# Attention weights times values: three fp32r passes on split operands instead of one fp32 matmul

## The chip, the cores and the metric

The kernel runs on one core of one Trainium2 chip. The metric is the device time of one execution in microseconds, the median of three runs.

## The reference

A backbone of two layers (DEPTH 2) over 1024 latent tokens and 256 context tokens, model width 1024, all in fp32. A layer norms and modulates the tokens, projects them, and runs three mixers side by side: attention, a Hyena long convolution and gated linear attention. Each head of each mixer is RMS-normed, all are concatenated and projected, and a SwiGLU follows. The attention has 8 query heads of 64 on 2 key/value heads:

```python
s = jnp.einsum('bqkgd,bskd->bkgqs', qg, k, preferred_element_type=jnp.float32)
p = jax.nn.softmax(s, axis=-1).astype(v.dtype)
o = jnp.einsum('bkgqs,bskd->bqkgd', p, v)
```

Latent queries read all 1280 keys, context queries the 256 context keys. In the last layer context queries aren't needed. What follows is `head_rms_norm` of `o`, so a common factor of a head's output matters only through the norm's epsilon.

## The kernel before

Each layer has three phases. Phase 1 norms, projects and prepares the mixers' inputs (queries, keys and values go to DRAM). Phase 2 (line 1372) runs the mixers. Phases 3 and 4 are the output projection and the SwiGLU. Instructions are not issued in the order of the source: a planner that simulates the engines sets each engine's order, with the tiles' dependencies and their buffers as limits. The source of phase 2 has the hyena first, then the linear attention, then the attention; the planner puts attention work among the other two.

The attention (lines 994 to 1104) goes job by job. A job is a key/value head (`kvh`), a pair of query heads (`pr`) and a block of queries: 512, 512, or 256 of the context. Layer 0 has 12 jobs, layer 1 has 8, all those of kv head 0 before those of kv head 1. `attn_kv` (line 995) loads the keys of one kv head and splits them: a high part in fp32r (an fp32 format with a shorter mantissa, which the matmul takes in one pass) and a low remainder. Kv head 0 is loaded at the end of phase 1 (line 770), kv head 1 when the first job needs it, into the pool `attn1`, which is open from the start of phase 2. `attn_q` splits the queries and finds each query's score maximum with extra matmuls and DVE reductions (line 1032). `attn_o` (line 1040) is the inner loop: per chunk of 128 keys and head, two fp32r matmuls make the scores (K1 with Q1, K2 with Q2), ACT takes the exponential (line 1057), and one plain fp32 matmul multiplies by the values (line 1060). The two heads' outputs go to partitions 0 to 63 and 64 to 127 of one PSUM bank. GpSimd adds the weights of all chunks (line 1068); after the last chunk fp32 matmuls with ones sum those over the partitions (line 1095). The block's end copies the output, squares it and the sums, adds them on DVE and norms (`headnorm`, line 977).

PSUM has eight banks, given to roles (line 1380): score maxima (0, 1, 2), scores (3, 4), outputs, sums and mean squares (5), the hyena and the linear attention (6, 7). Pools of SBUF are stacked on two sides. The right side holds `attn1`, `hna`, and on top of these the hyena's head norms `hn`; the hyena's other tiles are on the left. A pool opened later takes the room of one that has closed, and its tiles wait for the tiles that lay there.

Matmuls are all recorded at line 175, transposes at 184, low parts at 187.

Of the kernel before, what the change touches and what calls it, by code (L numbers as in the profile page):

```python
# [9 lines left out]
F32 = mybir.dt.float32  # L10
# [4 lines left out]
ALU = mybir.AluOpType  # L15
# [15 lines left out]
# columns of the combined input projection  # L31
C_Q, C_K, C_V, C_HY, C_GQ, C_GK, C_GV, C_GR, C_GF = 0, 512, 640, 768, 1536, 1664, 1792, 2048, 2304

# rows of the packed per-layer vectors
# [3 lines left out]
# ---------------------------------------------------------------- constants that depend on shapes alone  # L38
# [13 lines left out]
def _pk(m):  # L52
    """[T, K] -> [2, 128, T/128 * K]: exact parts, rows on partitions."""
    t, k = m.shape
    return np.stack([x.reshape(t // P, P, k).transpose(1, 0, 2).reshape(P, -1) for x in _hilo(m)])


def _consts():
# [27 lines left out]
    # rotations from the half-sample offset to offset 0, frequencies on partitions  # L86
# [37 lines left out]
class Builder:  # L124
# [21 lines left out]
    def ps(self, role=None):  # L146
        """a bank of PSUM: of a role, or of the current roles in turn."""
# [8 lines left out]
    def roles(self, *banks):  # L156
        """the banks of PSUM that each role takes in turn."""
        self.banks, self.turn = banks, [-1] * len(banks)

    def act_table(self, name):  # L160
        """one activation table set from here on: ScalarE's later instructions stay behind its load."""
# [11 lines left out]
    # -------------------------------------------------------------- small helpers  # L173
# [3 lines left out]
    def mm3(self, out, w, x, start, stop):  # L177
        """w, x: pairs (hi, lo); out += whi xhi + whi xlo + wlo xhi."""
        self.mm(out, w[0], x[0], start, False)
        self.mm(out, w[0], x[1], False, False)  # L180
        self.mm(out, w[1], x[0], False, stop)
# [7 lines left out]
    def rsqrt(self, pool, v, n, tag, eps=None, bufs=2):  # L189
        """-2 / sqrt(v + eps) for v [128, n] in PSUM: exp(-ln/2) and a Newton step."""  # L190
# [13 lines left out]
    # -------------------------------------------------------------- setup  # L204
# [42 lines left out]
    def vectors(self, vp, silb, ahead):  # L247
        """the conditioning vectors, biases and gains, features on partitions; other loads go ahead in between."""
        nc, A = self.nc, self.A
        for srcs in ((("c", None, 8), ("c_ctx", None, 8)),  # L250
# [22 lines left out]
            elif "filt_b1" in at:  # L273
                nc.vector.tensor_copy(self.fvec, ps[:, 0:3])
                # the norm gains scaled by -1/2: rsqrt() returns -2 / sqrt
# [6 lines left out]
    # -------------------------------------------------------------- adaLN vectors  # L282
# [10 lines left out]
    def ada_pe(self, l, part, wp, silb, ahead=()):  # L293
        """mod vectors: the conditioning vectors (16 columns each) stationary, weights moving; the rows of weights in
        turn on three column tiles."""
# [20 lines left out]
    def ada_dve(self, l, part, half, wp):  # L316
        """mod vectors of half a part: weighted rows summed on the vector engine; returns what sums the partitions."""
# [27 lines left out]
    # -------------------------------------------------------------- modulated norm: u (hi, lo) per block of tokens  # L345
    def norm_scale(self, l, which):
        """[128, 8, 2] gains: -1/2 g (1 + scale)."""
# [8 lines left out]
    def square(self, h, k, n, tp, acc):  # L356
        """adds the squares of chunk k of h [128, 8, n]; returns the sum so far, and whole, 1 / rms: tokens on partitions."""
# [23 lines left out]
    def spread(self, r, n, tp):  # L381
        """r [128, n / 128] -> -2 r of each token on all partitions, in PSUM."""
# [7 lines left out]
    def norm_u(self, h, u, scale, shift, r, tp, pool=(), tags=("s", "acc")):  # L390
        """u [128, 2, 8, n] F32R from h [128, 8, n]; r: -2 / rms; pool: the chunks whose low parts GpSimd makes."""
# [14 lines left out]
    # -------------------------------------------------------------- weights  # L406
    def load_w(self, src, n=P, wp=None, raws=None, lo_eng=None):
        """src [1024, n] -> (hi, lo) tile [128, 2, 8, n]."""
# [15 lines left out]
    # -------------------------------------------------------------- tokens in: feature-major residual  # L424
    def load_h(self, hp, xp):
        """features on partitions; yields after each block, with its -2 / rms on all partitions (PSUM)."""
# [35 lines left out]
    # -------------------------------------------------------------- hyena filters  # L462
    def sin_arg(self, pool, ps, b, fr, n):
        """sin(fr * (ps + b)) [128, n], the argument brought to [-pi, pi]."""
# [13 lines left out]
    def filter_mlp(self, fp, up):  # L478
        """hidden features of both layers' filters (a layer on 64 partitions), latent and context lengths, to DRAM."""
# [28 lines left out]
    def filter_body(self, l, kinds, fp):  # L508
        """spectra of one layer's filters to DRAM, latent ('l') and context ('c') lengths."""
# [5 lines left out]
        # X = [h_hi; h_lo], W1 = [w_hi; w_hi], W2 = w_lo  # L515
# [9 lines left out]
        def times(job):  # L525
            """the filter of a job in time, taken apart into folded levels."""
# [36 lines left out]
        def spectra(job, levels):  # L563
# [3 lines left out]
            for group in self.groups(levels):  # L567
                for pair, ps in self.transform(group, dft, fp):
                    for i, (L, k) in enumerate(pair):
# [20 lines left out]
                        else:  # L590
                            # cosine twice, or the two of the cyclic level; then the sine of either
# [26 lines left out]
    def start(self, hp, sp, up, tp, u):  # L618
        """tokens in, the first modulation vectors, the hidden features of the filters, the first norm."""
# [38 lines left out]
    # -------------------------------------------------------------- input projection  # L658
    def phase1(self, l):
        """norm 1, the input projection and what follows it token by token."""  # L660
# [3 lines left out]
        with ExitStack() as es:  # L664
# [27 lines left out]
            # feature-major columns  # L692
# [11 lines left out]
            # hyena: short convolution  # L704
# [21 lines left out]
            # gated linear attention: gates (silu as x sigmoid(x)), queries, keys  # L726
# [31 lines left out]
            with self.pool("t1q", 2, reuse_waits="tile") as tp:  # L758
# [5 lines left out]
                self.V = self.t(ap, [P, 10, P], F32, "V", 1)  # L764
                nc.sync.dma_start(out=self.V, in_=self.v_d)
# [8 lines left out]
    def open_w(self):  # L774
        """room of the streamed weights."""
# [8 lines left out]
    def open_u0(self):  # L784
        """room of the first block of the normed tokens."""
# [833 lines left out]
```

## Time and profile before

| | |
|---|---|
| median of three runs | 3708.47 us |
| lowest, highest | 3706.87, 3712.83 us |
| span of the profiled execution | 3712.2 us |
| PE busy | 3563.2 us (96%) |
| DVE busy | 2014.1 us (54%) |
| POOL busy | 1353.5 us (36%) |
| ACT busy | 1088.0 us (29%) |

No time of the profiled execution is given beside its span. A busy share is a mean over stages with different limits. PE is TensorE, PEld its weight loads, DVE VectorE, ACT ScalarE, POOL GpSimd, SP the engine that issues most DMAs. A plain fp32 matmul shows as two records.

### The profile page before, as it was taken

What the parts mean: (1) busy time and instruction counts of PE and PEld (TensorE: products, weight loads), DVE (VectorE), ACT (ScalarE), POOL (GpSimd) and SP (SyncE); (2) the same over time, 40 slices, a digit from 0 to 9 for tenths busy, and PEclk for the clock granted to TensorE, in tenths of its full rate; (3) what the DMA queues carried; (4) which work ended last, traced back from release to release, by engine and by line L of the source; (5) the groups of instructions that cost most, each with busy time, mean ns of one, the idle gap of its engine ahead of it and who ended that gap; (6) DMA issues with size and microseconds to landing.
All of it is one profiled execution on the core that took longest, in us unless ns stands there. A gap on an engine that the chain in (4) does not pass through costs nothing.

```text
span 3712.2 us, 46254 instructions
## 1 busy us (share of the span) xinstructions
PE 3563.2 (96%) x17903; PEld 2693.5 (73%) x17903; DVE 2014.1 (54%) x3271; ACT 1088.0 (29%) x1956; POOL 1353.5 (36%) x960
## 2 busy tenths in 40 slices
PE   8999899999999999999999899899999999999999
PEld 4789845445677888888888688865445788888887
DVE  6755667863677665644223773757753533223233
ACT  4243233553422111111111333333554421111112
POOL 2424564664333111111111541656764542221221
PEclk9999999999999999999999899999999999999999
DMA  9333311120633323321111333411112421111111
GB/s 329 99 124 123 120 33 43 56 81 20 212 110 99 95 80 89 90 66 54 49 35 46 107 111 116 150 49 42 35 70 71 139 63 51 40 57 46 52 40 57
DMA packets 275804, 310.63 MB, mean 84 GB/s; under 512 B 18680, under 2 KB 205727, under 8 KB 274304
## 3 DMA queue, kind: packets, MB, share of 16 engines
q1 hardware_dynamic: 269279, 287.75, 24.6%
q0 software_dynamic: 2560, 13.89, 1.0%
q10 hardware_dynamic: 3744, 6.03, 0.4%
q8 instruction: 140, 2.29, 0.3%
q14 instruction: 81, 0.66, 0.1%
HBM read 245.75 MB, written 61.87 MB: 83 GB/s over the span
## 4 chain that ended last, share of the span: by engine, by line
PE 75%; DVE 11%; POOL 4%; issue 3%; DMA 3%; ACT 1%; SPq 0%; DVEq 0%; POOLq 0%; ACTq 0%
PE ps L175 74%; PE ps L184 1%; POOL hss L928 1%; DMA nsq<-in_ada_w 1%; POOL hl L187 1%; DVE acc L329 1%; DVE mx L1032 1%; DVE sg L1138 1%; DMA yr<-y_d 0%; DVE h L1537 0%; POOL hy L936 0%; DVE sg L1150 0%; DVE sg L1151 0%; DVE nacc L365 0%; DVE hx L930 0%
## 5 line engine op out<-in xcount | busy, mean ns | idle before, releaser
L175 PE MATMUL ps<-u,hl 128*128 128x512 f32 (+1 forms) x6504 | 1384.4, 372 | 20.6 <-DVE u L403 6.2
L175 PEld LDWEIGHTS ps<-u,hl 128*128 128x128 f32 x6504 | 1136.3, 190 | 252.5 <-issue 14.9
L187 POOL TENSOR_TENSOR hl<-raw,hl 128x1024 fp32r<-128x1024 f32 x148 | 366.5, 2479 | 944.3 <-ACT hl L421 924.5
L175 PE MATMUL ps<-g,w 128*128 128x512 f32 (+1 forms) x2688 | 556.6, 367 | 10.0 <-DVE h L1537 3.4
L175 PEld LDWEIGHTS ps<-g,w 128*128 128x128 f32 x2688 | 466.6, 190 | 95.5 <-DVE h L1537 5.4
L1068 POOL TENSOR_TENSOR ac<-ac,p 128x512 f32<-128x512 f32 x256 | 354.7, 1394 | 159.4 <-ACT p L1057 158.8
L1498 DVE TENSOR_TENSOR s<-ps,s 128x512 f32<-128x512 f32 (+1 forms) x110 | 70.0, 637 | 614.7 <-PE ps L175 597.3
L1537 DVE SCALAR_TENSOR_TENSOR h<-ps,mod,h 128x512 f32<-128x512 f32 (+1 forms) x448 | 303.5, 687 | 181.8 <-PE ps L175 181.6
L175 PE MATMUL ps<-p,V 128*64 128x512 f32 x672 | 309.8, 607 | 4.7 <-ACT p L1057 2.5
L187 POOL TENSOR_TENSOR w<-raw,w 128x1024 fp32r<-128x1024 f32 x44 | 109.0, 2477 | 500.0 <-ACT w L421 499.9
L1032 DVE TENSOR_REDUCE mx<-ps 128x1 f32<-128x512 f32 (+1 forms) x400 | 221.0, 587 | 120.8 <-PE ps L175 119.8
L1057 ACT ACTIVATE p<-ps 128x512 f32<-128x512 f32 (+1 forms) x336 | 194.6, 586 | 286.8 <-PE ps L175 277.7
L175 PEld LDWEIGHTS ps<-Q,K 65*128 65x128 f32 (+1 forms) x672 | 105.0, 191 | 222.2 <-issue 209.8
L421 ACT CAST hl<-raw 128x1024 fp32r<-128x1024 f32 x148 | 154.9, 1049 | 303.9 <-PE ps L175 151.5
L329 DVE SCALAR_TENSOR_TENSOR acc<-nsq,silc,acc 128x512 f32<-128x512 f32 x252 | 210.6, 876 | 61.3 <-DMA nsq<-in_ada_w 60.6
L175 PE MATMUL ps<-Q,K 65*128 65x512 f32 (+1 forms) x672 | 242.2, 442 | 1.2 <-ACT p L1057 1.1
L175 PE MATMUL ps<-y,hl 128*128 128x512 f32 (+1 forms) x960 | 213.8, 381 | 13.2 <-DVE y L187 6.1
L175 PEld LDWEIGHTS ps<-y,hl 128*128 128x128 f32 x960 | 170.8, 194 | 59.3 <-DVE y L187 8.2
L421 ACT CAST w<-raw 128x1024 fp32r<-128x1024 f32 x44 | 46.2, 1051 | 491.8 <-PE ps L175 443.2
L175 PE MATMUL ps<-my,dft 128*128 128x256 f32 (+1 forms) x1176 | 166.8, 294 | 10.3 <-DVE my L187 9.7
L1499 ACT CAST g<-s 128x512 fp32r<-128x512 f32 (+1 forms) x110 | 63.3, 576 | 385.2 <-DVE s L1498 385.2
L175 PEld LDWEIGHTS ps<-my,dft 128*128 128x128 f32 x1176 | 159.1, 203 | 20.6 <-DVE my L187 13.7
(265 smaller groups left out, 4129.2 us busy)
## 6 DMA issues: line engine op xcount, KB each, us to landing
raw<-in_ffn_w SPq DMA_DIRECT2D x132, 512.0 KB
nsq<-in_ada_w SPq DMA_DIRECT2D x144, 256.0 KB
raw<-in_w_in SPq DMA_DIRECT2D x36, 512.0 KB
raw<-in_w_out SPq DMA_DIRECT2D x32, 512.0 KB
ada<-in_ada_w SPq DMA_DIRECT2D x24, 512.0 KB
h_d<-h SPq DMA_DIRECT2D x32, 256.0 KB
dft<-in_c_dft POOLq DMA_DIRECT2D x8, 1024.0 KB, 7.2
qd<-qT_d SPq DMA_DIRECT2D x64, 128.0 KB
```

The source lines that it names most:

```text
L175: self.nc.tensor.matmul(out, w, x, start=start, stop=stop)
L184: self.nc.tensor.transpose(out, in_, self.ident[:n, :n])
L187: eng.tensor_tensor(out=out, in0=x, in1=hi.bitcast(F32), op=ALU.subtract)
L329: nc.vector.scalar_tensor_tensor(out=acc[w], in0=raw, scalar=s, in1=acc[w], op0=ALU.mult, op1=ALU.add)
L421: self.nc.scalar.copy(hi, raw)
L928: nc.gpsimd.tensor_tensor(out=ss, in0=ss, in1=self.mh[:, :nh], op=ALU.pow)
L1032: nc.vector.tensor_reduce(out=mx[:, j, i:i + 1], in_=pm, op=ALU.max, axis=AX.X)
L1057: nc.scalar.activation(p, st, AF.Exp)
L1068: nc.gpsimd.tensor_tensor(out=acc[j], in0=x, in1=ps[j], op=ALU.add)
L1498: nc.vector.tensor_tensor(out=s, in0=p3, in1=s, op=ALU.mult)
L1499: nc.scalar.copy(gs[m][:, 0, o:o + n], s)
L1537: nc.vector.scalar_tensor_tensor(out=h, in0=ps, scalar=self.mod[l][:, 40 + k, w:w + 1], in1=h, op0=ALU.mult, op1=ALU.add)
```

## The change

The weights p are split: ACT copies p to an fp32r tile `ph`, GpSimd subtracts to give the low part `pl`. The values are split once a layer, into two tiles of 192 columns: the values of kv head 0, then 64 columns that hold ones in the high tile and zeros in the low one, then the values of kv head 1. A stationary operand of 128 columns is values beside ones (for kv head 1 ones beside values). Three fp32r passes accumulate, high by high, low values by high weights, high values by low weights, into one bank per head, whose other 64 partitions are the sum of the weights. GpSimd's sums and the ones matmuls are gone. The banks become (0, 1), (2, 3), (4, 5), (6, 7); the mean squares use role 0. The keys of kv head 1 go to a new pool `attn2`, opened after the hyena's pools have closed. Load buffers `qd` are two instead of three. The rest of the diff removes comments.

```diff
-                self.V = self.t(ap, [P, 10, P], F32, "V", 1)
-                nc.sync.dma_start(out=self.V, in_=self.v_d)
+                self.V = [self.t(ap, [P, 10, 192], F32R, f"V{i}", 1) for i in range(2)]
+                for i in range(2):
+                    nc.gpsimd.memset(self.V[i][:, :, 64:P].bitcast(F32), 1.0 - i)
+                for side, c in ((0, 0), (P, 64)):
+                    hi, lo = (x[:, :, side:side + 64] for x in self.V)
+                    for k in (0, 5):
+                        raw = self.t(ap, [P, 512], F32, "qd", 2)[:, :320].rearrange("p (k c) -> p k c", k=5)
+                        nc.sync.dma_start(out=raw, in_=self.v_d[:, k:k + 5, c:c + 64])
+                        self.split(raw, hi[:, k:k + 5], lo[:, k:k + 5], nc.vector)
...
-            raw = self.t(self.ap0, [P, 512], F32, "qd", 3)[:, :n]
+            raw = self.t(self.ap0, [P, 512], F32, "qd", 2)[:, :n]
...
-        return K1, K2, self.V[:, :, 64 * kvh:64 * kvh + 64]
+        return K1, K2, [x[:, :, 64 * kvh:64 * kvh + P] for x in self.V]
...
-        X = self.ps(2)[:, :n]
+        X = [self.ps(2)[:, :n] for _ in range(2)]
         k0 = 0 if b < 2 else 8
-        acc = [None, None]
...
-                p = self.t(ap, [P, 512], F32, "p", 6)[:, :n]
+                p = self.t(ap, [P, 512], F32, "p", 3)[:, :n]
+                hi, lo = (self.t(ap, [P, 512], F32R, x, i)[:, :n] for x, i in (("ph", 4), ("pl", 3)))
                 nc.scalar.activation(p, st, AF.Exp)
-                ps.append(p)
+                nc.scalar.copy(hi, p)
+                self.lo(nc.gpsimd, lo, p, hi)
+                ps.append((hi, lo))
             for j in range(2):
-                self.mm(X[64 * j:64 * j + 64], V[:, kc], ps[j], kc == k0, kc == 9)
+                self.mm(X[j], V[0][:, kc], ps[j][0], kc == k0, False)
+                self.mm(X[j], V[1][:, kc], ps[j][0], False, False)
             for j in range(2):
-                if kc == k0:
-                    acc[j] = ps[j]
-                    continue
-                x = acc[j]
-                if kc == k0 + 1:
-                    acc[j] = self.t(ap, [P, 512], F32, "ac", 2)[:, :n]
-                nc.gpsimd.tensor_tensor(out=acc[j], in0=x, in1=ps[j], op=ALU.add)
-        return X, acc
+                self.mm(X[j], V[0][:, kc], ps[j][1], False, kc == 9)
+        return X
...
-                ops[kvh] = self.attn_kv(ap, kvh)
+                ops[kvh] = self.attn_kv(self.ap1, kvh)
...
-            ps = self.ps(2)[:, :n]
+            ot = self.t(ap, [P, 512], F32, "ao", 2)[:, :n]
+            sq, e = (self.t(ap, [P, 512], F32, "sq", 2)[:, :n] for _ in range(2))
+            o, t = slice(64 * kvh, 64 * kvh + 64), slice(64 - 64 * kvh, P - 64 * kvh)
             for j in range(2):
-                self.mm(ps[64 * j:64 * j + 64], self.ones[:, :64], acc[j], True, True)
-            ot = self.t(ap, [P, 512], F32, "ao", 2)[:, :n]
-            nc.scalar.copy(ot, X)
-            sq, e = (self.t(ap, [P, 512], F32, "sq", 2)[:, :n] for _ in range(2))
+                h = slice(64 * j, 64 * j + 64)
+                nc.scalar.copy(ot[h], X[j][o])
+                nc.scalar.activation(e[h], X[j][t], AF.Square, scale=math.sqrt(EPS))
             nc.scalar.activation(sq, ot, AF.Square)
-            nc.scalar.activation(e, ps, AF.Square, scale=math.sqrt(EPS))
-            v = self.ps(2)[:, :n]
+            v = self.ps(0)[:, :n]
...
-            self.roles((0, 1, 2), (3, 4), (5,), (6, 7))
+            self.roles((0, 1), (2, 3), (4, 5), (6, 7))
...
+            self.ap1 = es.enter_context(self.pool("attn2", side="right", reuse_waits="tile"))
             self.open_w()
```

## Rows read from the trace of the kernel before

**Rows 1.** The page, parts 1, 2 and 4: busy times, tenths per slice, chain.
```profile
PE 3563.2 (96%) x17903; PEld 2693.5 (73%) x17903; DVE 2014.1 (54%) x3271; ACT 1088.0 (29%) x1956; POOL 1353.5 (36%) x960
PE   8999899999999999999999899899999999999999
PE 75%; DVE 11%; POOL 4%; issue 3%; DMA 3%; ACT 1%; SPq 0%; DVEq 0%; POOLq 0%; ACTq 0%
```

**Rows 2.** Busy us (xcount) of PE, PEld, DVE, ACT, POOL by stretch; clock, DMA share, GB/s.
```profile
445.00:800.00 355.00, 333.54 (x1322) 182.65 (x1321) 248.17 (x400) 147.46 (x284) 215.25 (x173) 0.95 0.15 45
800.00:960.00 160.00, 159.43 (x958) 81.37 (x958) 70.34 (x132) 71.10 (x157) 72.09 (x64) 0.99 0.16 55
2432.00:2695.00 263.00, 253.63 (x993) 135.75 (x991) 180.92 (x281) 108.98 (x197) 174.44 (x137) 0.99 0.13 40
2695.00:2860.00 165.00, 163.52 (x912) 78.05 (x911) 71.50 (x122) 77.39 (x159) 86.54 (x73) 1.00 0.13 47
```

**Rows 3.** The same stretches: ACT in exponentials (L1057) alone.
```profile
445.00:800.00 355.00, 68.81 (x120) 0.95 0.15 45
800.00:960.00 160.00, 31.20 (x56) 0.99 0.16 55
2432.00:2695.00 263.00, 55.54 (x94) 0.99 0.13 40
2695.00:2860.00 165.00, 39.02 (x66) 1.00 0.13 47
```

**Rows 4.** Timeline of PE, attention alone: start us, us, instructions merged.
```profile
804.91 0.74 PE L175 MATMUL ps<-Q,K 128*128 128x512 f32 x2
805.58 1.07 PE L175 MATMUL ps<-p,V 128*64 128x512 f32 x2
806.58 0.73 PE L175 MATMUL ps<-Q,K 128*128 128x512 f32 x2
```

**Rows 5.** Busy us in 50 us of SwiGLU, all matmuls fp32r of 512 columns.
```profile
3100.00:3150.00 50.00, 50.00 (x222) 41.42 (x221) 12.40 (x14) 9.75 (x13) 13.01 (x6) 1.00 0.21 64
```

**Rows 6.** Lines by form: busy us, mean ns | idle before, releasers.
```profile
L1068 POOL TENSOR_TENSOR ac<-ac,p 128x512 f32<-128x512 f32 x256 | 354.7, 1394 | 159.4 <-ACT p L1057 158.8
L175 PE MATMUL ps<-p,V 128*64 128x512 f32 x640 | 304.9, 618 | 4.2 <-ACT p L1057 2.5 <-DVE sq L1103 1.5
L1032 DVE TENSOR_REDUCE mx<-ps 128x1 f32<-128x512 f32 x256 | 170.5, 683 | 82.8 <-PE ps L175 81.9
L1032 DVE TENSOR_REDUCE mx<-ps 128x1 f32<-128x256 f32 x144 | 59.2, 415 | 38.0 <-PE ps L175 37.9
L187 POOL TENSOR_TENSOR my<-t,my 128x512 fp32r<-128x512 f32 x36 | 47.5, 1322 | 22.7 <-ACT my L1238 22.5
L175 PE MATMUL ps<-ac,ones 128*64 128x512 f32 x64 | 27.9, 631 | 0.0
L1025 ACT CAST Q<-qd 128x512 fp32r<-128x512 f32 x32 | 19.4, 617 | 18.9 <-PE ps L175 18.1 <-ACT hf L949 0.8
```

**Rows 7.** Timeline of PE, start of a job's values in layer 0.
```profile
909.56 2.80 PE L175 MATMUL ps<-p,V 128*64 128x512 f32 x12
```

**Rows 8.** Load of the values; value matmuls: ns min/median/max, first and last start.
```profile
L765 SPq DMA_DIRECT2D V<-v_d x2: 328/328/328, 359.7 to 2347.5; - x2
L175 PE MATMUL ps<-p,V x672: 379/592/1116, 466.8 to 2848.5; 128*64 128x512 f32 x160, 128*64 128x256 f32 x8
```

**Rows 9.** Timelines: keys of kv head 1 (SP); last hyena head norms (DVE).
```profile
574.70 14.21 SPq L1005 DMA_DIRECT2D qd<-kT_d  x6
...
800.58 1.38 DVE L991 SCALAR_TENSOR_TENSOR hyo<-sg,vecs,hr 128x256 f32<-128x256 f32 x1
...
2698.65 1.65 DVE L991 SCALAR_TENSOR_TENSOR hyo<-sg,vecs,hr 128x512 f32<-128x512 f32 x1
```

**Rows 10.** Busy us in two slices of layer 0's first stretch.
```profile
550.00:600.00 50.00, 44.81 (x196) 28.62 (x195) 44.96 (x63) 18.72 (x37) 28.46 (x24) 0.85 0.16 48
700.00:750.00 50.00, 44.16 (x169) 24.67 (x168) 46.37 (x88) 23.96 (x49) 21.14 (x19) 0.90 0.18 57
```

More of the change, by code (lines that the diff above doesn't have):

```diff
@@ L1016, in attn_q @@
         nt = n // P
-        raw = self.t(self.ap0, [P, 512], F32, "qd", 3)[:, :n]
+        raw = self.t(self.ap0, [P, 512], F32, "qd", 2)[:, :n]
         for j in range(2):
@@ L1040, in attn_o @@
     def attn_o(self, ap, ops, b, Q):
+        K1, K2, V = ops
         nc = self.nc
-        K1, K2, V = ops
         n = BLK[b][1]
-        X = self.ps(2)[:, :n]
+        X = [self.ps(2)[:, :n] for _ in range(2)]
         k0 = 0 if b < 2 else 8
-        acc = [None, None]
         for kc in range(k0, 10):
@@ L1089, in attention @@
             nxt = queries(i + 1)
-            X, acc = self.attn_o(ap, ops[kvh], b, Q)
+            X = self.attn_o(ap, ops[kvh], b, Q)
             Q = nxt
-            ps = self.ps(2)[:, :n]
+            ot = self.t(ap, [P, 512], F32, "ao", 2)[:, :n]
+            sq, e = (self.t(ap, [P, 512], F32, "sq", 2)[:, :n] for _ in range(2))
+            o, t = slice(64 * kvh, 64 * kvh + 64), slice(64 - 64 * kvh, P - 64 * kvh)
             for j in range(2):
-                self.mm(ps[64 * j:64 * j + 64], self.ones[:, :64], acc[j], True, True)
-            ot = self.t(ap, [P, 512], F32, "ao", 2)[:, :n]
-            nc.scalar.copy(ot, X)
-            sq, e = (self.t(ap, [P, 512], F32, "sq", 2)[:, :n] for _ in range(2))
+                h = slice(64 * j, 64 * j + 64)
+                nc.scalar.copy(ot[h], X[j][o])
+                nc.scalar.activation(e[h], X[j][t], AF.Square, scale=math.sqrt(EPS))
             nc.scalar.activation(sq, ot, AF.Square)
-            nc.scalar.activation(e, ps, AF.Square, scale=math.sqrt(EPS))
-            v = self.ps(2)[:, :n]
+            v = self.ps(0)[:, :n]
             self.mm(v, self.blk, sq, True, True)
```

## Prediction

> **What bounds the kernel now.** The page comes first: TensorE (PE) is busy 96% of the span, and 75% of the chain of waits is PE [rows 1]. An average over all stages doesn't say what the attention is worth, so the busy time by stretch comes next. The attention shares the middle of each layer with two other mixers. I cut each layer's middle within 6 us of the hyena's last head norm, since the change ties something to that point. Stretch A is from the start to there (355 us in layer 0, 263 us in layer 1), stretch B from there to the output projection (160 and 165 us). PE is busy 94 to 100% of all four, VectorE (DVE) 69 to 70% of the two A, 43 to 44% of the two B; ScalarE (ACT) and GpSimd (POOL) are at 41 to 66% [rows 2]. So PE sets the pace, with DVE next in the A. The exponentials, one per unit of attention (a chunk of 128 keys, one head, 512 queries), show where the attention stands: 120 and 56 units in layer 0, 94 and 66 in layer 1 [rows 3].
>
> **TensorE per unit.** Where nothing but attention runs, PE alternates two score matmuls with one plain fp32 value matmul, which shows as two records: 804.91, 805.58, 806.58, so 0.67 us and 1.00 us, 1.67 us a unit [rows 4]. The new unit is five fp32r passes. Bounds of one pass of 512 columns: 222 matmuls in 50 us of a pure fp32r stage is 0.225 us [rows 5]; next to an fp32 matmul a score pass costs 0.335 us (half of 0.67). Five passes are 1.13 to 1.68 us. I take 1.15, near the first, because all five neighbours become fp32r with all 128 columns. Gain 0.52 us x 320 units = 166 us; the 16 units of 256 queries give about 4. The ones matmuls over the sums go: 27.9 us for the 64 wide ones [rows 6]. Together some 198 us of PE work for the two layers, if PE were all that counted.
>
> Here a rule speaks against the change. Of 12 value-matmul records queued together, six matmuls took 2.80 us, 0.47 us each: there the two heads, on the two column halves, ran over each other [rows 7]. Alone, one takes 1.00 us [rows 4]. The Trainium skill, "TensorE: Matmul & The Clock Gate", section "Part 3: Packing small matmuls — row/col tiling", says that matmuls on different column tiles run concurrently; the trace agrees where they are adjacent. By that rule the old pair would cost 0.94 us and the new one, which takes all columns, 1.35. But the 640 wide records keep PE busy 304.9 us [rows 6], 0.95 us a matmul, against 150 us were all overlapped. So this is a rival, not the sum.
>
> **ScalarE.** A cast of 128x512 to fp32r takes 0.617 us [rows 6]: 320 of them and 16 at about 0.4 are 204 us more over the two layers. The job's end goes from three reads to five (two heads' outputs, two heads' squares on 64 partitions, one square): 1.2 us a job, 24 us for 20 jobs.
>
> **GpSimd.** The sums that go (256 at 1.394 us, 40 more, about 404 us) are replaced by 336 subtractions. The same operation for another tile takes 1.322 us [rows 6]: 436 us. The change's "no GpSimd sums" frees nothing on GpSimd, and the latency from exponential to the last pass grows by a copy and a subtraction, 1.94 us.
>
> **The banks.** The score-maximum matmuls have two banks instead of three. DVE needs 0.683 us per reduction of 512 [rows 6], PE 0.225, so two banks feed it as well as three; I count 0, and up to 40 us if each third wait of the 120.8 us (82.8 + 38.0) that DVE sat idle before those reductions doubles [rows 6]. A bank per head instead of one for outputs, sums and mean squares: the next job's values wait for two short reads and no longer for the DVE addition. The 12 queued records are such a backlog [rows 7], but PE had other work then. I take 0; at most 3 us x 20 jobs gained.
>
> **Values split.** Four small loads, copies and DVE subtractions a layer take the place of one load at 359.7 us [rows 8], a hundred us ahead of the first value matmul at 466.8. The queue of SP and the two instead of three load buffers are shared with the first keys; I count 0 with that cover, 10 us a layer without.
>
> **The second kv head moves.** K1 and K2 of kv head 1 now come from a pool that is opened on the same side after the hyena's head-norm pool has closed, so in its room: their first write waits for the hyena's last head norms. Those are at 800.58 in layer 0 [rows 9]. Before, their loads went out at 574.70 [rows 9], in the middle of the hyena. The loads, ACT's casts and DVE's subtractions of the keys, the query loads of the next job and its score maxima queue behind this wait, and all exponentials of kv head 1 stand behind those. So stretch A can hold no more than kv head 0: 88 units instead of 120 in layer 0, 80 instead of 94 in layer 1. The rest goes to B.
>
> **The sum by stretch.**
> A of layer 0: PE 333.5 - 194 (120 old units) + 97 (88 new) - 9 (maxima of 1.6 jobs) - 8 (ones) = 220 us. DVE 248.2 - 23 (1.6 jobs, each 16 reductions of 0.683 and 8 of 0.415 [rows 6]) = 225. DVE is late next. Its share is 70% now and 90 to 93% in two slices of 50 us, 550 to 600 and 700 to 750 [rows 10]. I take 80% between: 281 us, so -74.
> B of layer 0: PE 159.4 - 87 - 5 + 97 + 9 = 173, and 12 us of the start of kv head 1 that the linear attention doesn't fill: 185, +25.
> A of layer 1: PE 253.6 - 157 + 92 - 4 - 8 = 177; DVE 180.9 - 10 = 171, at 80% 214: -49.
> B of layer 1: PE 163.5 - 110 - 6 + 92 + 4 = 144; ACT 77.4 - 39 + 98 (80 units of 1.22) + 9 (0.7 of a job at ten reads of about 0.6, and four longer job ends) = 145, so these two are level; 152 with their waits and 20 us of start: 172, +7.
> Together -91. PE is then only some 80% busy in A, and in the slice 550 to 600, where it had 44.8 of 50, the granted clock was 0.85 [rows 10], part of it at the lower of 1.2 and 2.4 GHz. I give back 10 us for that and 10 for the edits counted at 0: -71. The profiled span is 3712.2 us; no further time of that execution is given, and it lies 3.7 above the median. 3712.2 - 71 - 3.7 is 3637; I say 3640.
>
> **The rivals.**
> *PE's gain comes out whole.* PE is over 94% busy in all stretches, which speaks for it. DVE's 248 of 355 us speaks against, and so do the 88 and 80 units that B must hold. 198 us less the two starts of 20: 3712 - 158 - 4, about 3550.
> *The second kv head comes too late (slower).* The hyena is a chain of DVE, GpSimd and PE work. If that chain and not PE sets its end, A shrinks by 10 us each, and B holds 32 and 14 more units at ACT's pace: layer 0's ACT 71.1 - 31.2 + 104 + 17 = 161, at 80% 201, and 20 of start is +61; layer 1's 145 at 80% and 20 is +36. +77 in all, 3712 + 77 - 4: 3785. It decides from the point where both hyena ends come less than about 16 us earlier each, half of the 32 by which I let the B grow. For it: DVE operations of the hyena stand in the slices where PE idles. Against: 120 units of 1.67 us, 200 us of PE, lie among the hyena's matmuls in A of layer 0, and in the new kernel 101.
> *The pace stays.* Exponential 0.59 (39.02 / 66 [rows 3]), copy 0.62, subtraction 1.32 on two score banks and three p tiles: if PE waits for each unit's low part, a unit stays at 1.67. Three tiles over 2.5 us allow 0.85 us a unit, which speaks against. About 3705.
> *The heads already overlap.* By rows 7 the new unit would cost 0.21 us more, x 320 = 67: 3775. Against it the 0.95 us a matmul above.
>
> **How the numbers follow.** Forecast 3640 with a range of its own of 3590 to 3690: 0.60. Whole gain 0.16, second head late 0.15, pace stays 0.06, overlap 0.03. To hold 8 in 10 the range reaches into the first two: 3550 to 3740. Two versions that differ by less than 0.2%, 7.4 us, can't be told apart here (three runs lie within 6 us). Faster: the first two, 0.76; the same: 0.05 of the paced case; slower: the rest, 0.15 + 0.03 + 0.01 = 0.19.
>
> **What would show it.** Right: fp32r value passes at 0.225 to 0.24 us; units 1.15 us of PE where attention runs alone; no exponentials of kv head 1 before the hyena's last head norm, and that norm 75 and 50 us earlier in its stretch; GpSimd's attention work above 404 us; DVE above 75% in A. Wrong: the hyena's end unmoved with PE idle in A, or B longer by over 60 us; value passes above 0.33 us; the kv head 1 keys still loaded in mid-hyena.

## The result, and the profile after

The changed kernel takes 3826.02 us (median of 4 runs, 3824.74 to 3839.06) against 3710.65 us of the kernel before (median of 4 too): a ratio of 1.0304, 95% interval 1.0278 to 1.033. It is 3% slower; the forecast was 71 us faster. The profiled span is 3837.3 us, 125 us above the 3712.2 of before (115 by the medians: the profiled execution of after is the longest of its four).

The page after, busy time by engine, PE's tenths and the granted clock per slice [rows 1]:

```profile
PE 3568.7 (93%) x18159; PEld 2890.3 (75%) x18159; DVE 2039.3 (53%) x3279; ACT 1291.8 (34%) x2340; POOL 1396.6 (36%) x1004
PE   7999888698989999999999899888799999999999
PEclk9999988768989999999999899999779999999999
```

PE's busy time is the same as before, but with holes above all in slices 5 to 8 and 26 to 29, where the two layers have their mixers; the clock falls to 0.6 to 0.8 in slices 6 to 10 and to 0.7 in 29 and 30. Stretches A and B again, busy us (xcount) of PE, PEld, DVE, ACT, POOL, then clock [rows 2]; and below them ACT in exponentials alone [rows 3]:

```profile
445.00:749.00 304.00, 249.85 (x1194) 194.29 (x1194) 211.70 (x336) 170.25 (x330) 192.42 (x161) 0.89 0.15 46
749.00:1044.00 295.00, 263.22 (x1290) 183.60 (x1291) 138.71 (x222) 165.47 (x334) 132.76 (x107) 0.79 0.17 55
2503.00:2748.00 245.00, 212.42 (x1023) 167.59 (x1023) 169.01 (x246) 140.38 (x258) 170.84 (x137) 0.93 0.13 40
2748.00:3003.00 255.00, 230.03 (x1171) 162.96 (x1170) 122.77 (x188) 153.34 (x292) 130.09 (x101) 0.83 0.18 58
```
```profile
445.00:749.00 304.00, 50.20 (x88) 0.89 0.15 46
749.00:1044.00 295.00, 50.15 (x88) 0.79 0.17 55
2503.00:2748.00 245.00, 47.12 (x80) 0.93 0.13 40
2748.00:3003.00 255.00, 47.24 (x80) 0.83 0.18 58
```

All of kv head 1 (88 and 80 units) stands behind the hyena, as forecast. The hyena's last head norm in layer 0 is at 748.86 instead of 800.58 [rows 9], so A is 52 us shorter. In layer 1 the last one of before is not the one of rows 9 (2698.65) but a later one, 2707.59; after has it at 2747.99. Layer 1 starts 77 us later in after, so A is 37 us shorter there. (The stretches of layer 1 in [rows 2] part 13 us ahead of that norm, so their lengths don't give this.) The lines are of before, after and after:

```profile
2707.59 0.73 DVE L991 SCALAR_TENSOR_TENSOR hyo<-sg,vecs,hr 128x512 f32<-128x512 f32 x1
748.86 0.49 DVE L999 SCALAR_TENSOR_TENSOR hyo<-sg,vecs,hr 128x256 f32<-128x256 f32 x1 [0.52 <-DMA y_d<-hyo]
2747.99 1.66 DVE L999 SCALAR_TENSOR_TENSOR hyo<-sg,vecs,hr 128x512 f32<-128x512 f32 x1
```

But B of layer 0 runs to 1036, where the last exponential is (before: 952).

The new unit on PE where its neighbours are only attention [rows 4]; then the lines that answer to [rows 6]:

```profile
972.02 0.39 PE L175 MATMUL ps<-K,Q 128*128 128x512 f32 x1
972.25 0.63 PE L175 MATMUL ps<-Q,K 128*128 128x512 f32 x2
972.72 0.63 PE L175 MATMUL ps<-ph,V 128*128 128x512 f32 x2
973.18 0.39 PE L175 MATMUL ps<-pl,V 128*128 128x512 f32 x1
973.41 0.40 PE L175 MATMUL ps<-K,Q 128*128 128x512 f32 x1
```
```profile
L1066 ACT CAST ph<-p 128x512 fp32r<-128x512 f32 x320 | 194.9, 622 | 5.2
L187 POOL TENSOR_TENSOR pl<-p,ph 128x512 fp32r<-128x512 f32 x320 | 443.2, 1407 | 280.8 <-ACT ph L1066 183.7 <-PE ps L175 58.9 <-issue 34.9
L1040 DVE TENSOR_REDUCE mx<-ps 128x1 f32<-128x256 f32 x144 | 60.0, 418 | 77.1 <-PE ps L175 76.4
L175 PE MATMUL ps<-pl,V 128*128 128x512 f32 x320 | 137.6, 434 | 13.6 <-POOL pl L187 13.1
```

Five passes start 0.23 us apart (972.25 to 973.41, 1.16 us). The copy costs what was forecast (0.622 us, forecast 0.617), the subtraction 6% more (1.407, forecast 1.322). So the prices of the single new operations held, and the 125 us are in how the parts meet.

**Where the time is.** I took each kernel's two middles: from 445 us to the last matmul of the output projection in layer 0, and from 1344 us behind that to the same matmul in layer 1. The 1344 us between are common. The view is busy time by stretch, first of before, then of after:

```profile
445.00:1102.00 657.00, 623.15 (x2904) 366.04 (x2904) 428.96 (x682) 266.13 (x516) 334.67 (x259) 0.96 0.25 79
2446.00:2964.00 518.00, 499.18 (x2238) 278.30 (x2238) 310.10 (x461) 227.20 (x411) 315.69 (x240) 0.99 0.21 66
```
```profile
445.00:1179.00 734.00, 630.93 (x3042) 470.74 (x3043) 449.87 (x692) 373.37 (x721) 361.66 (x285) 0.85 0.23 72
2523.00:3089.00 566.00, 504.04 (x2425) 377.72 (x2424) 328.41 (x469) 323.91 (x590) 338.24 (x257) 0.89 0.20 63
```

Idle is length less PE's busy time. "Half clock" is half of the busy time that lies in clock records of 0.50: what those matmuls would have saved at the upper level. The rest is PE's work at full clock. "Behind" counts the units of attention (exponentials) after the last matmul of the linear attention, layer 0 / layer 1. A is the part of both middles up to the start of the hyena's last head norm, B the part from there on. Kernels by that working, each from its one profiled execution, us:

```
kernel                         both middles  idle  half clock  work  behind     A    B
before                             1175       53       28      1094   0 / 0    617  559
after                              1300      165      140       995  63 / 67   528  773
x1  before, late keys              1305      126       84      1095  60 / 63   546  759
x12 before, all banks changed      1286       77       59      1150  34 / 32   580  706
x13 before, two maxima banks       1284       89       61      1134  24 / 20   587  698
x3  after, smaller hyena room      1299      165      134       999  67 / 66   532  768
x2  x3 with early keys             1203      126       81       996  43 / 32   534  669
x9  after, low part not read       1269      158      123       988  65 / 64   528  741
x6  after, no subtraction          1193      109       92       992  67 / 65   462  731
x7  x2, no subtraction             1156      100       56      1000  44 / 39   478  679
x4  after, no low part             1146      113      126       907  67 / 67   439  708
x11 after, filler matmuls          1288      166       84      1038  67 / 64   528  760
x5  early keys, no low part, copy  1085       98       67       919  44 / 39   461  624
```

From before to after PE's work falls by 99 us; idle time takes 112 of it back and the clock another 112: 125 us more. By part, A is 89 us shorter and B 214 us longer. And before, no attention is left when the linear attention ends; after, 130 units are.

### The profile page after: what moved, and what is told of

Its sections match the earlier page's. It is cut to its first block, busy times and chain, and to the rows that moved or that the text cites. A ratio compares the mean times of both kernels' runs of the same rounds, so it can differ in the third digit from the quotient of the medians.

```text
span 3837.3 us, 47299 instructions
## 1 busy us (share of the span) xinstructions
PE 3568.7 (93%) x18159; PEld 2890.3 (75%) x18159; DVE 2039.3 (53%) x3279; ACT 1291.8 (34%) x2340; POOL 1396.6 (36%) x1004
## 5 line engine op out<-in xcount | busy, mean ns | idle before, releaser
L187 POOL TENSOR_TENSOR pl<-p,ph 128x512 fp32r<-128x512 f32 (+1 forms) x336 | 454.7, 1375 | 296.5 <-ACT ph L1066 197.4
L1040 DVE TENSOR_REDUCE mx<-ps 128x1 f32<-128x512 f32 (+1 forms) x400 | 229.3, 589 | 155.3 <-PE ps L175 153.9
L175 PE MATMUL ps<-y,hl 128*128 128x512 f32 (+1 forms) x960 | 222.3, 385 | 23.4 <-DVE h L1570 10.9
L175 PE MATMUL ps<-Q,K 65*128 65x512 f32 (+1 forms) x672 | 229.2, 425 | 3.8 <-ACT p L1065 2.7
L175 PE MATMUL ps<-ph,V 128*128 128x512 f32 x672 | 222.9, 421 | 9.0 <-ACT sq L1104 8.0
L175 PE MATMUL ps<-K,Q 128*128 128x512 f32 (+1 forms) x400 | 169.2, 446 | 40.0 <-DVE mx L1040 34.2
L1066 ACT CAST ph<-p 128x512 fp32r<-128x512 f32 (+1 forms) x336 | 201.1, 612 | 5.4
```

What stands on the lines that cost most here:

```text
L175: self.nc.tensor.matmul(out, w, x, start=start, stop=stop)
L187: eng.tensor_tensor(out=out, in0=x, in1=hi.bitcast(F32), op=ALU.subtract)
L1040: nc.vector.tensor_reduce(out=mx[:, j, i:i + 1], in_=pm, op=ALU.max, axis=AX.X)
L1066: nc.scalar.copy(hi, p)
```

## The experiments

Each run stands beside runs of the kernel before on the same chip; a ratio times 3715 us is used to set runs of different chips beside each other. The edits are shown in part; `...` stands for lines left out.

**Late keys (x1 to x3).** The first edit on the kernel before; the second on the changed one, where the keys of kv head 1 fit early only if the hyena's pool shrinks; the third is that smaller room alone.

```diff
 x1 (before)   +  self.ap1 = es.enter_context(self.pool("attn2", side="right", ...))   # after the hyena
               -  ops[kvh] = self.attn_kv(ap, kvh)
               +  ops[kvh] = self.attn_kv(self.ap1, kvh)
 x2 (after)    -  HYB = {1024: 6, 512: 4, 256: 8, "my": 6, "spec": 3, "t": 2}
               +  HYB = {1024: 6, 512: 4, 256: 7, "my": 5, "spec": 2, "t": 2}
               -  ops[kvh] = self.attn_kv(self.ap1, kvh)
               +  ops[kvh] = self.attn_kv(ap, kvh)
 x3 (after)       the HYB line of x2 alone
```

> The kernel before with one part of the change alone: the keys of kv head 1 come from a pool opened after the hyena. Theory L (the late second kv head costs the time): 3780 to 3830 us, no exponential of kv head 1 before the hyena's last head norm, and a stretch at the lower clock behind it. Rival G (ScalarE's copies and GpSimd's subtractions pace the attention): no difference from before, 3700 to 3725. Rival B (two score-maximum banks instead of three): 3700 to 3725 too.

> The changed kernel with the keys of kv head 1 in the pool that is open from the start, as before the change; to make room the hyena has one buffer less for my (5), spec (2) and the 256 wide signal (7). Theory L: 3620 to 3690 us, about 150 below the changed kernel, with exponentials of kv head 1 inside the hyena. Rival G: above 3780. Rival B: above 3780.

> The changed kernel, keys late, with the same three hyena buffers less: what the missing buffers cost by themselves. All theories: 3826 plus 0 to 20 us. If it is more than 20, the early keys have to be compared with this kernel and not with the changed one.

Measured: x1 3849.23, ratio 1.0359 (1.0339 to 1.0378): the late keys alone cost 133 us, more than the whole slowdown, and more than theory L's range. In the table, A is 71 us shorter, as 46 units leave it, and B 200 us longer. x2 3738.31, 1.0051 (1.0036 to 1.0066); x3 3841.49, 1.0328 (1.0309 to 1.0346). With the room equal, early keys give back 103 us, nearly all of it in B by the table (768 to 669), but x2 isn't faster than before, though its PE has 98 us less to do: theory L's range (3620 to 3690) is missed too. Something else is in it. ACT's exponentials by stretch, first while the linear attention runs, then behind it, of x1 and of x2; then of after, beginning with the 37 us before the first one of kv head 1:

```profile
766.00:900.00 134.00, 16.57 (x28) 0.83 0.15 47
900.00:1042.00 142.00, 34.01 (x60) 0.96 0.16 49
```
```profile
761.00:893.00 132.00, 25.08 (x44) 0.93 0.13 43
893.00:985.00 92.00, 24.59 (x43) 0.91 0.21 68
```
```profile
749.00:786.00 37.00, 0.00 (x0) 0.50 0.47 167
786.00:898.00 112.00, 14.60 (x25) 0.74 0.07 23
898.00:1037.00 139.00, 35.55 (x63) 0.90 0.18 55
```

Before, the linear attention ran from 814 to 958 with 49 units beside it, and the attention was done first. With late keys 28 and 25 units lie beside it, and 60 and 63 behind it, where PE has little else: in after, 14 us of the output projection in 139 us.

**The low part (x4, x6, x7, x8, x9).** x4 drops pass and subtraction; x6 keeps the pass, on the high part; x7 is x6 with early keys and x2's room; x8 is x2 with the subtraction on VectorE; x9 makes the subtraction and lets nobody read it. In x6, x7 and x9 the third pass counts the high part twice; in x4 a part of the product is left out. x4, x6 and x7 also have seven `ph` tiles instead of four, in the room of `pl`; x9 has four.

```diff
 x4, x6, x7  -  hi, lo = (self.t(ap, [P, 512], F32R, x, i)[:, :n] for x, i in (("ph", 4), ("pl", 3)))
             +  hi = self.t(ap, [P, 512], F32R, "ph", 7)[:, :n]
 x4  -  self.lo(nc.gpsimd, lo, p, hi)
     -  self.mm(X[j], V[0][:, kc], ps[j][1], False, kc == 9)
     ...
 x6, x7  -  self.lo(nc.gpsimd, lo, p, hi)
         -  ps.append((hi, lo))
         +  ps.append((hi, hi))
 x8  -  self.lo(nc.gpsimd, lo, p, hi)
     +  self.lo(nc.vector, lo, p, hi)
 x9  -  ps.append((hi, lo))
     +  ps.append((hi, hi))
```

> The changed kernel without the low parts of the weights: no GpSimd subtraction and no third value pass (that part of the product is left out). Theory L: GpSimd's 455 us and a third of the value passes go with little effect, 3770 to 3830. Rival G: below 3720. Rival B: 3800 to 3830.

> The changed kernel with three value passes, but the third takes the rounded weights again instead of their low part, so that no subtraction is made on GpSimd (the output counts the weights twice there). Keys late as in the changed kernel. Theory TensorE pays (336 passes of 0.26 us are 88 us, the rest of the 141 us is GpSimd's): 3765 to 3800. Rival GpSimd paces (the pass is free, the subtraction was the cost): 3685 to 3725.

> As the run with early keys and a smaller room of the hyena (3738), but the third pass takes the rounded weights again and no subtraction is made (the output counts the weights twice there). Theory TensorE pays: GpSimd's wait is worth 20 to 50 us at most, 3690 to 3720. Rival GpSimd paces: 3600 to 3660.

> As the run with early keys and a smaller room of the hyena (3738), but the subtraction is made by VectorE instead of GpSimd; nothing is left out. Theory VectorE is late next beside the hyena (some 230 us more on an engine that was the last releaser of most of TensorE's waits): 3740 to 3790. Rival GpSimd paces: the half as long subtraction gives back 30 to 70 us, 3670 to 3710.

> The changed kernel with its 336 GpSimd subtractions, but the third pass reads the rounded weights again and nobody reads the low part, so that no value matmul waits for GpSimd (the output counts the weights twice there). Theory occupation (the subtractions cost by GpSimd's time, by the exponentials that wait for their p tile and by VectorE's operations, which take longer beside them): near the changed kernel, 3800 to 3840. Rival latency (the third pass waits for the low part): near the run without subtractions (3738), 3735 to 3765.

Measured: x4 3684.66, 0.9908 (0.9894 to 0.9923); x6 3738.25, 1.0062 (1.0038 to 1.0086); x7 3694.46, 0.9939 (0.9916 to 0.9961); x8 3721.55, 1.0016 (0.9997 to 1.0035); x9 3798.05, 1.0215 (1.0193 to 1.0237). Without the subtraction the changed kernel is 90 us faster (x6), with early keys 42 (x7 against x2); the third pass is worth another 57 (x6 to x4), of 86 us of PE's work. x4 lies in the range of rival G, so the low part does cost. x6 lies between its two theories: neither TensorE's pass nor GpSimd alone. x8 lies between its two as well and decides for neither; on VectorE the subtraction costs 13 us less than on GpSimd. x9 tells the two ways of GpSimd apart: of the 90 us, 33 go when no matmul waits for the low part, and 57 stay, by occupation. The table puts them in different places: the wait in B (773 to 741), the occupation in A, which is 528 in after and x9 and 462 in x6. Whatever the three more `ph` tiles of x6 are worth is in these 57 us too. ACT stood idle 5.2 us in all before the 320 wide copies of after (above), so few of them can have waited for a tile; whether more tiles changed the planned order wasn't tried. How GpSimd costs without being waited for is seen on VectorE: the same line with two inputs in SBUF, of before, after and x6 (no subtraction):

```profile
L201 DVE SCALAR_TENSOR_TENSOR hr<-hr,hr 128x512 f32<-128x512 f32 x32 | 29.7, 928 | 0.5
```
```profile
L201 DVE SCALAR_TENSOR_TENSOR hr<-hr,hr 128x512 f32<-128x512 f32 x32 | 36.1, 1130 | 0.4
```
```profile
L201 DVE SCALAR_TENSOR_TENSOR hr<-hr,hr 128x512 f32<-128x512 f32 x32 | 22.4, 701 | 0.5
```

Over all, VectorE is busy 2039.3 us in after and 1950.8 in x6, with the same 3279 instructions: 88 us on an engine of the hyena's chain. A score-maximum reduction, which reads PSUM, takes 0.69 us in both. Of x6:

```profile
PE 3519.0 (94%) x18159; PEld 2868.1 (77%) x18159; DVE 1950.8 (52%) x3279; ACT 1279.0 (34%) x2340; POOL 949.6 (25%) x668
```

The Trainium skill, "SBUF — State Buffer", section "SBUF: two separate sides", says that GpSimd and VectorE lock a common port pair for a whole instruction, and that an operation of VectorE with two SBUF inputs needs it; the three rows of L201 agree. Before, with GpSimd's sums, the line took 928 ns, and VectorE was busy 2014.1 us over all: the change did not bring this, it kept it and added some.

**The order behind the hyena, and the clock (x10, x11).** x10 writes the rest of the attention ahead of the linear attention. x11 adds filler matmuls to the linear attention.

```diff
 x10    with self.pool("gla", 1, reuse_waits="tile") as gp:
     +      self.role = None
     +      for _ in self.attention(l, last, ap, npa): pass
     +      self.role = 3
     ...
 x11 +  for z in range(4):  self.mm(ps[:, 320:512], K1[:, :P], K1[:, :192], True, True)
     +  for z in range(12): self.mm(po[:, 256:512], K1[:, :P], K1[:, :256], True, True)
```

> The changed kernel with the rest of the attention written ahead of the linear attention in each layer, so that kv head 1, once its keys are there, goes first and the linear attention fills TensorE's gaps; nothing is left out. Theory (units of attention that stand alone at the end, at GpSimd's pace, are the loss): 3770 to 3805. Rival (the keys' arrival and the half clock before it are the loss, and the order behind them doesn't matter): 3815 to 3840.

> The changed kernel with filler matmuls in the linear attention, on the keys of kv head 0, into columns that nobody reads: four of 192 columns at each of the 18 states and twelve of 256 at each output tile of a layer, some 37 us of TensorE at full clock over both layers (estimated from 0.225 us for 512 columns). Theory (the half clock of some 95 and 75 us before kv head 1 is a loss of its own, and TensorE gets full clock back when it is kept busy): the two stretches at 0.50 go, 3785 to 3820. Rival (the clock is a companion of waiting for the keys, nothing ends sooner by it): 3830 to 3870.

Measured: x10 3856.55, 1.0384 (1.0355 to 1.0412): my theory missed, the units behind fall only to 54 and 59, and it is slower, above the rival's range too. x11 3827.23, 1.0305 (1.0282 to 1.0328), no change, between its two ranges. PE's windows of the two long stretches at half clock, after and then x11:

```profile
730.00:826.00 96.00, 71.17 (x416) 46.61 (x415) 40.63 (x86) 26.42 (x73) 14.45 (x16) 0.50 0.25 86
2751.00:2827.00 76.00, 66.17 (x395) 42.42 (x396) 31.81 (x61) 21.32 (x59) 8.49 (x12) 0.51 0.26 88
```
```profile
733.00:829.00 96.00, 73.95 (x548) 56.82 (x549) 41.18 (x89) 31.17 (x79) 16.42 (x18) 0.70 0.26 87
2754.00:2830.00 76.00, 66.67 (x548) 51.06 (x548) 39.01 (x74) 31.63 (x76) 13.14 (x16) 0.84 0.28 93
```

The clock did come back (0.70 and 0.84), and the loss to it fell by 56 us; but the fillers are 43 us of work, and the linear attention of layer 0 ended at 894 instead of 898. So whether the half clock is a price by itself isn't settled: in this form, what it gives back is spent.

**The banks (x12, x13).** All banks of the change on the kernel before, then only the score maxima's.

```diff
 x12 -  self.roles((0, 1, 2), (3, 4), (5,), (6, 7))
     +  self.roles((0, 1), (2, 3), (4, 5), (6, 7))
 x13 +  self.roles((0, 1), (2, 3, 4), (5,), (6, 7))
```

> The kernel before with the banks of the changed one alone: two instead of three for score maxima, two instead of one for outputs and mean squares; no other edit. By the prediction 0, at most 40 us slower: 3715 to 3725 is its 0, 3755 its bound. Rival (the output bank that no longer waits for the addition of the last job is worth something by itself): 3690 to 3710.

> The kernel before with score maxima on two banks instead of three, and scores on three instead of two; one bank for outputs, two for the hyena, as before. Theory maxima (the third bank for maxima is what lets a job's preparation run ahead of the hyena's work, so that attention ends before the linear attention): near the run with all banks changed (3820), 3790 to 3830, and some 30 units of each layer left behind the linear attention. Rival outputs (the second output bank changes the order): 3710 to 3735.

Measured: x12 3819.64, 1.0277 (1.0255 to 1.0298); x13 3829.48, 1.0303 (1.028 to 1.0326). One bank taken from the maxima costs the kernel before 103 to 113 us by itself. Exponentials of x13 beside and behind the linear attention, and of before for the same places:

```profile
801.00:955.00 154.00, 24.02 (x43) 0.89 0.06 21
955.00:1023.00 68.00, 12.90 (x24) 1.00 0.30 89
```
```profile
814.00:958.00 144.00, 26.46 (x49) 0.99 0.10 29
958.00:1036.00 78.00, 0.00 (x0) 0.96 0.85 269
```

The linear attention ends at the same time (955, 958), and the hyena's last transform starts even earlier (763 instead of 781), but attention had 92 units done by then instead of 111. The reductions fall behind too: the 200th of layer 0's 208 ends at 963 instead of 865. PE itself waits little for them (25 us before score-maximum matmuls against 17, both layers); the order of its instructions is another, with the hyena's matmuls where maxima stood. That two banks bound how early the planner can place them, and that this and no wait on the chip is the cost, is argued from this, not shown.

A third of this price can't be carried over to the changed kernel. Of the 111 us by which x12's middles grow, 56 are PE's work (1094 to 1150), and 33 of these, at full clock, lie in the plain fp32 value records: their mean from start to next start is 0.48 us instead of 0.43. Of x12, against 304.9 us in [rows 6]:

```profile
L175 PE MATMUL ps<-p,V 128*64 128x512 f32 x640 | 349.8, 636 | 4.4 <-ACT p L1057 3.8 <-ACT sq L1100 0.3
```

The changed kernel has no such records.

**Giving the bank back (x14 to x17).** The maxima share a bank with the scores, or take one from them.

```diff
 x14 (on x5), x15 (on x2)  +  self.roles((0, 1, 2), (2, 3), (4, 5), (6, 7))
 x16 (on x2), x17 (on x5)  +  self.roles((0, 1, 2), (3,), (4, 5), (6, 7))
```

> The run with the exponentials straight into fp32r, two value passes and early keys (3623), with a third bank for score maxima that they share with the scores; the weights still have no low part. Theory maxima: its 44 and 39 units behind the linear attention shrink, 3560 to 3600. Rival outputs: unchanged, 3610 to 3635; a shared bank that blocks the scores: slower than 3635.

> The changed kernel with early keys in the smaller room (3738) and with a third bank for score maxima that they share with the scores; nothing is left out. Theory maxima: 3670 to 3705, faster than the kernel before. Rival outputs: unchanged, 3730 to 3750; a shared bank that blocks the scores: slower than 3750.

> The changed kernel with early keys in the smaller room (3738) and with three banks of their own for score maxima, as before, at the price of one bank instead of two for the scores; nothing is left out. Theory maxima (the bank alone costs 115 us in the kernel before): a job's preparation runs ahead again, units behind the linear attention fall from 43 and 32 towards 0, 3650 to 3710. Rival single score bank (a score and its exponential follow each other, 0.46 and 0.60 us and two handovers, so a unit takes 1.3 to 1.6 us everywhere): 3740 to 3800.

> The run with the exponentials straight into fp32r, two value passes and early keys (3623) with the same banks: three for maxima, one for scores; the weights have no low part. Theory maxima: 3560 to 3600. Rival single score bank: 3640 to 3720.

Measured: x14 3736.25, 1.0052 (1.0036 to 1.0068); x15 3914.47, 1.0527 (1.0508 to 1.0546); x16 3770.51, 1.0156 (1.0122 to 1.0191); x17 3661.49, 0.9871 (0.9829 to 0.9913). All are slower than their bases: with a bank shared with the scores, all of kv head 1 is left behind the linear attention (88 and 80 units in x14); one score bank leaves 65 and 50 (x16). A layout with three for maxima and two for each of the others needs nine banks. Taking one from the hyena wasn't tried, since it holds two at once. So no run shows what the bank costs in the changed kernel.

**A faster kernel (x5).** The exponential writes fp32r itself: no copy, no low part of the weights, two passes. So it leaves a part of the product out. The room this frees takes the keys early with the hyena's full buffers.

```diff
 -  p = self.t(ap, [P, 512], F32, "p", 3)[:, :n]
 ...
 -  nc.scalar.activation(p, st, AF.Exp)
 -  nc.scalar.copy(hi, p)
 -  self.lo(nc.gpsimd, lo, p, hi)
 +  nc.scalar.activation(hi, st, AF.Exp)
 ...
 -  ops[kvh] = self.attn_kv(self.ap1, kvh)
 +  ops[kvh] = self.attn_kv(ap, kvh)
```

> The weights are rounded to fp32r by the exponential itself and have no low part: no copy, no subtraction, two value passes instead of three; the room this frees takes the keys of kv head 1 early, with all buffers of the hyena as in the kernel before. Theory two causes (TensorE pays for the third pass, and the late keys cost idle time and clock, each by itself): 3685 of the run without the low part, less 88 to 132 for the early keys: 3555 to 3600. Rival one cause (without the low part, the late keys are hidden, as GpSimd was what made them late): 3650 to 3690.

Measured: 3622.85 us, 0.9752 (0.973 to 0.9774): faster than both. That is above the range of "two causes": the gains overlap. There are still 44 and 39 units behind the linear attention; that the two maxima banks leave them there is likely from x12 and x13, not shown:

```profile
719.00:842.00 123.00, 24.36 (x43) 0.91 0.13 44
842.00:925.00 83.00, 25.14 (x44) 0.90 0.23 72
```

## Why the prediction was wrong

By stretch, the sum had A shorter by 123 us and B longer by 32, for both layers. A came out shorter by 89 and B longer by 214. So B is the step that failed (129 us longer in layer 0, 85 in layer 1); the prediction had named over 60 as a sign of being wrong. With the late keys alone (x1) B is already 200 longer and A 71 shorter.

- **The second kv head** (B +25 and +7; as a rival +61 and +36). The step that failed. That kv head 1 would stand behind the hyena, exponentials and all, was right, but the term was mis-sized: alone it costs 133 us on the kernel before (x1), and early keys give 103 back on the changed one (x2 against x3). I filled B with units at a pace and 12 to 20 us of start, as if the linear attention lay beside them. In fact keys are cast from 751 on, the first exponential follows at 786 and the second at 828, and 63 of 88 units stay behind the linear attention, which until 826 ran almost alone and at half clock. The rival "too late" (3785) had the sign, and too low a price.
- **The banks** ("two banks feed it as well as three; I count 0, and up to 40 us"). On the kernel before the term is 103 to 113 us (x12, x13). I priced a bank by the pace of the engines on its two sides. It may also bound how far ahead a job's preparation can be ordered; that order let the attention of layer 0 end 6 us before the linear attention. How much of it is in the changed kernel's time stays open.
- **TensorE per unit** (198 us). PE's work fell by 99. The new unit alone is 1.16 us, as forecast. But the old one was priced where attention stood alone, 1.67 us [rows 4], and most of it did not: summed from start to next start at full clock, over all 336 units, the value records of before cost 0.43 us each and the score passes 0.30, so 1.45 us a unit; the new unit averages 1.23. Two value records are 0.86 where I took 1.00 and [rows 7] showed 0.47: the rival "heads overlap" held for about a quarter. In x12 the same records cost 0.48 each. This mean was in the trace of before.
- **GpSimd** ("frees nothing"; nothing added for latency). Its 454.7 us are near the 436 forecast, but not free: 42 us with early keys, 90 with late ones. Two thirds of the 90 are occupation, and it shows in the hyena's part.
- **Stretch A** (DVE at 80%). VectorE was at 70% (211.70 of 304) and 69% (169.01 of 245), as before, and PE idled 54 us of 304: neither engine was full. 52 and 37 us came instead of 74 and 49. Without the subtractions (x6) the two A are 155 us shorter than before, so their occupation took some 66 us of A.
- **The clock** (10 us given back for it and the slack). 112 us, with idle time of the same size. Of the clock's loss 95 us lie in B, most of it in the two long stretches in which the linear attention ran before kv head 1; idle time grew by 56 us in A and 56 in B.
- Right: the price of each new pass, copy and subtraction; the values' split is hidden (first exponential at 473 us against 464, and x13 without the split has 469); no exponential of kv head 1 before the hyena's last head norm.

The pieces don't add: late keys (133) and the bank (103 to 113) each leave units behind the linear attention, and together hardly more than the keys alone (63 / 67 against 60 / 63). By the ratios after is 113 us slower: what the keys alone cost, less 20, although PE has 99 us less to do. The subtraction's 90 is inside that. I found no sum of separate prices that gives it. What is shown is that late keys alone make either kernel over 100 us slower; why the changed kernel with early keys (x2) still isn't faster than before is shown only for the 42 us of the subtraction.

## What to carry to other kernels

When an engine is 96% busy because three streams lie side by side, price a change by what it does to their order: count what is left of each stream when the others end. A buffer or bank that "feeds as well with two as with three" may be the look-ahead that keeps the streams level; undo such a line alone before trusting a zero, in the new kernel as well as in the old one. Price an operation by its mean over the program, not where it is easiest to see.

## What the hardware showed that was not expected

TensorE ran at 0.50 of its clock, 1.2 GHz, for 95.6 us from 730.7 although its records were busy 71.17 of 96 us, most of that with small matmuls of the linear attention; before, the same matmuls beside the attention had 0.99. And 336 GpSimd subtractions cost VectorE 88 us, on the same instructions, and the hyena's part some 66 us, whether or not a matmul waited for them (x9).
